# A list scheduler's durations for matmuls and DMA are replaced in a two-layer decoder trunk

## The chip, the cores and the metric

The kernel runs on one core of a Trainium2 chip. The metric is the device time of one execution in microseconds. Before the change the median of three runs is 997.61 us (995.69 to 997.91). One further execution was profiled; its numbers below are from that profile.

## The reference

A trunk of two layers works on one sequence of 256 tokens with 1024 channels in float32. Each layer is a half-step SwiGLU FFN, a token mixer and a second half-step FFN. The mixer of layer 0 is stick-breaking attention with 16 heads, that of layer 1 a gated linear recurrence (RG-LRU) with a width of 1280. Before each of the six sub-layers the input is normalized, scaled and shifted, and the result of the sub-layer is gated; scale, shift and gate come from a conditioning vector through a large matrix `mod_w` (2 layers x 1024 x 9216).

```python
c_act = jax.nn.silu(c)
for layer in range(DEPTH):
    mod = (c_act @ mod_w[layer] + mod_b[layer]).reshape(B, N_SUB, 3, D_MODEL)
    h, g = sublayer_input(x, norm_g[layer, 0], mod[:, 0])
    x = x + MACARON_W * g * swiglu(h, ffn_w_gu[layer, 0], ffn_w_down[layer, 0])
    h, g = sublayer_input(x, norm_g[layer, 1], mod[:, 1])
    ...
    x = x + g * y
    h, g = sublayer_input(x, norm_g[layer, 2], mod[:, 2])
    x = x + MACARON_W * g * swiglu(h, ffn_w_gu[layer, 1], ffn_w_down[layer, 1])
return rmsnorm(x, final_norm_g)
```

`sublayer_input` is `rmsnorm(x, g) * (1 + scale) + shift`. The weights are read once: some 250 MB, of which the conditioning matrix is 75 MB.

## The kernel before

*Arithmetic.* A product of float32 operands is made of three matmuls: each operand is split into a rounded high part and the remainder, and high x high, high x low and low x high are added up in PSUM. `Acc.group` (L514 to L534) issues such a group of three, all at L526: 128 x 128 weights against 256 tokens. A few products take float32 directly, in one instruction of four passes (`group32`, L543; the recurrence's gates, L1033; the sums of squares, L608).

*Weights.* They come in chunks of 1 MB (128 x 2048), which feed 16 groups. `load` (L482) reserves one of 3 `raw` buffers and issues the DMA (L472, on the SyncE queue). Then it splits the chunk in two halves of 1024 columns: ScalarE writes the high part `wh` (L497), VectorE the remainder `wl` (L500). There are 7 half-chunk buffers of either kind.

*Conditioning.* `mod_w` is not multiplied on TensorE. It is cut into 18 vectors (2 layers x 3 sub-layers x shift, scale, gate) of 8 tiles of 128 x 1024, 0.5 MB each: 144 tiles. `mod_tile` (L553) loads one into one of 3 `rawm` buffers, and VectorE multiplies it by `silu(c)` and sums along the row, in one instruction and a read of the accumulator (L564). When the 8 tiles of a vector are there, `mod_final` makes the shift (L577), the scale (L579, L582) or the gate (L579, L585). The 16 tiles of the first scale and shift go with the first weights. All others stand in a list in the order in which they are needed, beginning with the first gate, then the scale, shift and gate of attention, then the scale and shift of the second FFN: tiles 57 to 64 are that shift. `hook` (L1189) takes them off the list as the program is written down: in the first FFN 1.5 for every chunk of the up projection from the eighth on, and as much for every position of the down part, whose steps are two positions apart. A tile may be loaded, by the plan, once the last TensorE operation that was written down before it is done. That dependency orders the plan alone; on the chip a load waits for its buffer.

*Stages.* Each FFN has an up projection (22 chunks), then a down projection (`down`, L643, 11 chunks), whose last part finishes the eight 128-channel blocks of x one after the other: a residual addition (L666), a square (summed at L601) and a scaled copy `hx` of x, split again (`scaled`, L616 to L627). The next sub-layer begins with these copies (`up_first`, L705), before the sum of squares is known; two more columns carry the shift (L624), and the evictions apply the norm afterwards (L722, L723). So the first matmuls of a sub-layer need its scale and its shift. Attention works in eight pairs of heads: projections (L526, L836), masked scores (L900 and the paired products L912), a chain on ScalarE and VectorE, sums (L937, L939), values (L959), and then a down part of 4 chunks.

*The planner.* The program is written down as operations with an engine, a duration and buffers. `Program.schedule` (L165) then plays it through once, on the host, before anything is issued. Every operation gets a priority, its latest start by the durations of what depends on it; TensorE operations start from the running sum of their own durations (`nominal`, L115). The engine that can start first takes its most urgent operation; ScalarE and VectorE may hold still a little for a more urgent one that is about to become ready (`wait_for`, L227). A buffer is given out again when the plan says that its last user is done. At the end all operations are sorted by their planned start and issued in that order. The five queues, SyncE's DMA queue among them, are then worked off strictly in order, and semaphores keep the data right. A planned duration thus never delays an instruction by itself: it only decides what stands before what in each queue. The durations come from `c_act`, `c_dve`, `c_mm` and `c_dma` (L348 to L361), the delays between engines from the tables at L101 to L103. A DMA occupies the plan's single DMA engine for `c_dma` and lands 2000 ns (950 ns in the first loads) after that.

Of the kernel before, what the change touches and what calls it, by code (L numbers as in the profile page):

```python
# [14 lines left out]
P = 128  # L15
T = 256
# [337 lines left out]


def c_mm(n, passes=3):
    return passes * (max(n, 256) / 2.4 + 2.5)


def c_dma(n):  # L360
    return n * P * 4 / 360.0 + 20.0  # L361


@with_exitstack
def trunk(ctx, tc, xT, cb, par, modw, gu0, gu, wdn, qk, wv, wo, win, wri, wout, out):
# [3 lines left out]
    pr = Program()  # L369
# [101 lines left out]
    def dma(dst, src, n, w, after=(), lat=None):  # L471
        return pr.op("DMA", c_dma(n), lambda: sp.dma_start(dst(), src), w=w, after=after, lat=lat)  # L472

    def A(o, i, f, n, r, w, table=None, psum=False, ptr=0, after=(), **kw):
        def fn():
            act.activation(o(), i(), f, **{k: (v() if callable(v) else v) for k, v in kw.items()})  # L476
        return pr.op("ACT", c_act(n, psum, ptr), fn, r, w, after, table)

    def V(fn, n, r, w, cost=None, ptr=0):
        return pr.op("DVE", cost or c_dve(n) + 62.0 * ptr, fn, r, w)  # L480
# [26 lines left out]
    class Acc:  # L507
# [6 lines left out]
        def group(self, part, o, w, wc, xs, xc, stop, parts=(None,), passes=(0, 1, 2)):  # L514

            b = self.b
            start = not self.started
            self.started = True
            wh, wl = w
            xh, xl = xs  # L520

            def fn():
                seq = ((wh, xh), (wh, xl), (wl, xh))
                for n, i in enumerate(passes):
                    u, v = seq[i]
                    pe.matmul(o(b()), wc(u()), xc(v()), start=start and n == 0, stop=stop and n == len(passes) - 1,  # L526
                              skip_group_check=True)

            n = xs_n[0]
            rd = [wh, wl] + [(t, q) for t in (xh, xl) for q in parts]  # L530
            if not start:
                rd.append((b, "start"))
            wr = [(b, part)] + ([(b, "start")] if start else [])
            return pr.op("PE", c_mm(n, len(passes)), fn, rd, wr)  # L534
# [3 lines left out]
    def group32(acc, part, o, w, wc, x32, xc, n, stop):  # L538

        b = acc.b  # L540
        start = not acc.started
        acc.started = True
        pr.op("PE", c_mm(n, 4), lambda: pe.matmul(o(b()), wc(w()), xc(x32()), start=start, stop=stop, skip_group_check=True),  # L543
              [w, x32] + ([] if start else [(b, "start")]), [(b, part)] + ([(b, "start")] if start else []))
# [58 lines left out]
    def rstd(gen):  # L603
        qs = ssq.pop(gen)
        qs = qs if isinstance(qs, tuple) else (qs,)
        b = Buf(banks)
        for i, q in enumerate(qs):
            pr.op("PE", c_mm(T, 4), lambda i=i, q=q: pe.matmul(b()[:, :T], ones, q(), start=i == 0, stop=i == len(qs) - 1),  # L608
                  [q] + [b] * (i > 0), [b])
        r = Buf(rmsr)  # L610
        o = Buf(rstr)
        A(r, lambda: b()[:, :T], AF.Ln, T, [b], [r], table="lnexp", psum=True, ptr=1, bias=eps_t, scale=1.0 / D)
        A(o, r, AF.Exp, T, [r], [o], table="lnexp", scale=-0.5)
        return o
# [123 lines left out]
    def split(y, a, n):  # L738
        A(y[0], a, AF.Copy, n, [a], [y[0]])
        V(lambda: dve.tensor_tensor(y[1](), a(), f32(y[0]()), ALU.subtract), n, [a, y[0]], [y[1]])  # L740
# [66 lines left out]
    def attention(l, s, nxt, hook):  # L807
# [78 lines left out]
        def hd(ap, e):  # L886
            return ap[:, e * S : (e + 1) * S]

        def scores(f):

            qh, ql = qs.pop(f)
            zs[f] = Buf(banks), Buf(banks)
            u = Buf(F, 6, name=f"u{f}")

            def masked(e):
                b = zs[f][e]

                def fn():
                    diag = b().rearrange("p (e t) -> p e t", e=2)[:, :, :P]
                    pe.matmul(diag, ident, mask.rearrange("p (e t) -> p e t", e=2), start=True, stop=False,  # L900
                              skip_group_check=True)
                pr.op("PE", c_mm(T, 1), fn, [], [b])

            zb = zs[f]

            def products():

                for i, (kc, qc) in enumerate(((slice(T, T + P), slice(0, T)), (slice(T + P, 2 * T), slice(P, T)))):
                    for n, (v, w) in enumerate(((qh, qh), (qh, ql), (ql, qh))):
                        for e in range(2):  # L910
                            rows = slice(e * 64, (e + 1) * 64)
                            pe.matmul(zb[e]()[:, BL[i]], v()[rows, kc], w()[rows, qc], start=False,  # L912
                                      stop=i == 1 and n == 2, skip_group_check=True)

            for e in range(2):
                masked(e)
            pr.op("PE", 2 * c_mm(T), products, [qh, ql], list(zb))
            for e in range(2):
                A(lambda e=e: hd(u(), e), lambda b=zs[f][e]: b()[:, :S], AF.Abs, S, [zs[f][e]], [(u, e)], psum=True)
            A(u, u, AF.Exp, W2, [u], [u], table="lnexp", scale=-1.0)  # L920
            A(u, u, AF.Ln, W2, [u], [u], table="lnexp", bias=1.0)
            for e in range(2):
                V(lambda e=e, b=zs[f][e]: dve.scalar_tensor_tensor(hd(u(), e), b()[:, :S], 0.0, hd(u(), e), ALU.max, ALU.add),
                  S, [zs[f][e], (u, e)], [(u, e)])
            y = ws_[f] = Buf(R, 6, name=f"sh{f}"), Buf(R, 6, name=f"sl{f}")
            split(y, u, W2)
# [49 lines left out]
        for f in range(8):  # L976
            hook(f)
            q_proj(f)
            if f >= 2:
                values(f - 2)  # L980
            if f in (0, 1, 3, 5):
                v_proj((f + 1) // 2)
            if f >= 1:
                sums(f - 1)
            scores(f)
# [141 lines left out]
    def final():  # L1127
        q = rstd("end")

        def put(d0, n):  # L1130
            o = xall[:, d0 * T : (d0 + n) * T].rearrange("p (d t) -> p d t", d=n)
            V(lambda: dve.tensor_tensor(o, o, q().unsqueeze(1).to_broadcast([P, n, T]), ALU.mult), n * T,
              x[d0 : d0 + n] + [q], x[d0 : d0 + n])
            pr.op("DMA", c_dma(n * T), lambda: sp.dma_start(out[:, d0 : d0 + n, :], o), x[d0 : d0 + n], [])

        for d0, n in ((0, 1), (1, 1), (2, 2), (4, 2), (6, 1), (7, 1)):
            put(d0, n)
# [137 lines left out]
```

## Time and profile before

| | |
|---|---|
| runs, median | 997.61 us (995.69 to 997.91) |
| profiled execution | 996.92 us, span 994.8 us |
| mean granted TensorE clock | 0.996 |
| first group of the FFN (L526) | 13.7 us after the start |
| end of TensorE's last group | 986.0 us |
| DMA | 251.24 MB, 253 GB/s on average |
| conditioning tiles (L564) | 144, mean 1220 ns and 84 ns for the accumulator |
| wl splits (L500) | 328, mean 1210 ns |

Times within the profile count from its first instruction. PE is TensorE, PEld its weight load, DVE VectorE, ACT ScalarE, SPq the SyncE queue that issues all DMAs. The profile calls PE busy from a matmul's start to its modelled end, and those overlap; so how dense TensorE runs is better seen from the number of matmuls in a stretch of time than from its busy share. Durations of single instructions on VectorE overlap their successors a little, too: two L500 in a row take 2.35 us.

### The profile page before, as it was taken

What the parts mean: (1) busy time and instruction counts of PE and PEld (TensorE: products, weight loads), DVE (VectorE), ACT (ScalarE), POOL (GpSimd) and SP (SyncE); (2) the same over time, 40 slices, a digit from 0 to 9 for tenths busy, and PEclk for the clock granted to TensorE, in tenths of its full rate; (3) what the DMA queues carried; (4) which work ended last, traced back from release to release, by engine and by line L of the source; (5) the groups of instructions that cost most, each with busy time, mean ns of one, the idle gap of its engine ahead of it and who ended that gap; (6) DMA issues with size and microseconds to landing.
All of it is one profiled execution on the core that took longest, in us unless ns stands there. A gap on an engine that the chain in (4) does not pass through costs nothing.

```text
span 994.8 us, 19695 instructions
## 1 busy us (share of the span) xinstructions
PE 976.2 (98%) x8096; PEld 964.5 (97%) x8096; DVE 799.0 (80%) x1316; ACT 562.3 (57%) x902; POOL 2.2 (0%) x14
## 2 busy tenths in 40 slices
PE   6999999999999999999999999999999999999997
PEld 5999999999999899999999999999999999999996
DVE  7997888798888999888789988874997996555433
ACT  5475453478785754445366544443779785444333
POOL 0000000000000000000000000000000000000000
PEclk9999999999999999999999999999999999999999
DMA  8988899835556499889866888985244645555431
GB/s 332 352 325 315 331 333 330 334 136 203 198 206 236 170 341 336 331 327 341 326 246 253 329 327 333 343 324 212 108 134 164 254 175 209 204 175 186 166 115 43
DMA packets 48331, 251.24 MB, mean 253 GB/s; under 512 B 5489, under 2 KB 6129, under 8 KB 28530
## 3 DMA queue, kind: packets, MB, share of 16 engines
q1 hardware_dynamic: 48242, 249.99, 68.5%
q8 instruction: 63, 1.03, 0.4%
q14 instruction: 26, 0.21, 0.1%
HBM read 248.92 MB, written 1.05 MB: 251 GB/s over the span
## 4 chain that ended last, share of the span: by engine, by line
PE 95%; DVE 2%; DMA 1%; issue 0%; ACT 0%; SPq 0%; DVEq 0%
PE bank L526 89%; PE bank L836 2%; PE bank L1033 1%; PE bank L959 1%; DVE rawm L564 1%; PE bank L543 1%; PE bank L912 1%; PE bank L937 1%; DMA rawm<-in_modw 1%; DMA x<-in_xT 0%; PE bank L608 0%; PE bank L939 0%; DVE ssq L601 0%; DVE wl L500 0%; DVE x L666 0%
## 5 line engine op out<-in xcount | busy, mean ns | idle before, releaser
L526 PE MATMUL bank<-hx,wh 128*128 128x256 f32 (+1 forms) x3392 | 610.2, 283 | 5.1 <-ACT hx L476 4.8
L526 PEld LDWEIGHTS bank<-hx,wh 128*128 128x128 f32 x3392 | 522.3, 189 | 8.2 <-ACT hx L476 5.7
L497 ACT ACTIVATE wh<-raw 128x1024 fp32r<-128x1024 f32 (+1 forms) x328 | 336.8, 1046 | 340.1 <-PE bank L526 228.6
L500 DVE TENSOR_TENSOR wl<-raw,wh 128x1024 fp32r<-128x1024 f32 (+1 forms) x328 | 390.0, 1210 | 133.2 <-ACT wh L497 130.0
L526 PE MATMUL bank<-hx,wl 128*128 128x256 f32 (+1 forms) x1696 | 476.3, 281 | 0.0
L526 PEld LDWEIGHTS bank<-hx,wl 128*128 128x128 f32 x1696 | 321.2, 189 | 0.3 <-DVE wl L500 0.3
L526 PE MATMUL bank<-arenar,wh 128*128 128x256 f32 x1664 | 294.3, 280 | 0.0
L526 PEld LDWEIGHTS bank<-arenar,wh 128*128 128x128 f32 x1664 | 254.0, 188 | 0.1
L526 PE MATMUL bank<-arenar,wl 128*128 128x256 f32 x832 | 232.5, 279 | 0.0
L564 DVE SCALAR_TENSOR_TENSOR rawm<-rawm,cact 128x1024 f32<-128x1024 f32 x144 | 174.5, 1220 | 10.2 <-DMA rawm<-in_modw 10.0
L526 PEld LDWEIGHTS bank<-arenar,wl 128*128 128x128 f32 x832 | 156.3, 188 | 0.0
L476 ACT ACTIVATE arenar<-a 128x256 fp32r<-128x256 f32 x88 | 35.2, 404 | 4.9 <-DVE a L735 4.8
L740 DVE TENSOR_TENSOR arenar<-a,arenar 128x256 fp32r<-128x256 f32 x88 | 36.4, 419 | 0.5 <-ACT arenar L476 0.5
L735 DVE TENSOR_TENSOR a<-bank,sg 128x256 f32<-128x256 f32 x82 | 34.2, 419 | 0.1
L476 ACT ACTIVATE sg<-bank 128x256 f32<-128x256 f32 x82 | 30.2, 368 | 5.2 <-PE bank L526 1.7
L666 DVE SCALAR_TENSOR_TENSOR x<-bank,mf,x 128x256 f32<-128x256 f32 x48 | 22.1, 480 | 11.8 <-PE bank L526 11.6
L476 ACT ACTIVATE hx<-hpre,mf 128x256 fp32r<-128x256 f32 x48 | 23.2, 503 | 13.6 <-DVE mf L577 6.6
L476 ACT ACTIVATE hx<-x,mf 128x256 fp32r<-128x256 f32 x40 | 19.3, 504 | 20.3 <-DVE x L666 20.2
L636 DVE SCALAR_TENSOR_TENSOR hx<-hpre,mf,hx 128x256 fp32r<-128x256 f32 x48 | 22.8, 482 | 1.3 <-ACT hx L476 1.3
L634 DVE SCALAR_TENSOR_TENSOR hpre<-x,mf,rst 128x256 f32<-128x256 f32 x48 | 21.9, 482 | 2.3 <-ACT rst L476 1.9
L836 PE MATMUL bank<-wh,hx 128*128 128x256 f32 x128 | 23.7, 283 | 0.0
L476 ACT ACTIVATE arenaf<-arenaf 128x768 f32<-128x768 f32 (+1 forms) x31 | 21.9, 735 | 0.3
(97 smaller groups left out, 452.6 us busy)
## 6 DMA issues: line engine op xcount, KB each, us to landing
raw<-in_gu SPq DMA_DIRECT2D x79, 1024.0 KB, 4.9
rawm<-in_modw SPq DMA_DIRECT2D x144, 512.0 KB, 5.9
raw<-in_wdn SPq DMA_DIRECT2D x44, 1024.0 KB, 5.0
raw<-in_win SPq DMA_DIRECT2D x10, 1024.0 KB, 4.7
raw<-in_qk SPq DMA_DIRECT2D x8, 1024.0 KB, 4.8
raw<-in_gu SPq DMA_DIRECT2D x14, 512.0 KB, 6.7
raw<-in_wout SPq DMA_DIRECT2D x5, 1024.0 KB, 5.0
raw<-in_wv SPq DMA_DIRECT2D x4, 1024.0 KB, 4.7
```

Of the source, the lines that this page charges most:

```text
L476: act.activation(o(), i(), f, **{k: (v() if callable(v) else v) for k, v in kw.items()})
L497: act.activation(h()[:, :m], raw()[:, a : a + m], AF.Copy)
L500: dve.tensor_tensor(lo()[:, :m], raw()[:, a : a + m], f32(h()[:, :m]), ALU.subtract)
L526: pe.matmul(o(b()), wc(u()), xc(v()), start=start and n == 0, stop=stop and n == len(passes) - 1, skip_group_check=True)
L543: pr.op("PE", c_mm(n, 4), lambda: pe.matmul(o(b()), wc(w()), xc(x32()), start=start, stop=stop, skip_group_check=True), [w, x32] + ([] if ...
L564: dve.scalar_tensor_tensor(raw(), raw(), 1.0, cact(), ALU.mult, ALU.mult, accum_out=m()[:, t : t + 1])
L634: V(lambda: dve.scalar_tensor_tensor(hp(), x[d](), gs()[:, c], q(), ALU.mult, ALU.mult), T, [x[d], (gs, d), q], [hp], ptr=1)
L636: V(lambda: dve.scalar_tensor_tensor(lo()[:, :T], hp(), sh()[:, c], f32(hi()[:, :T]), ALU.add, ALU.subtract), T, [hp, (sh, d), hi], [lo], ...
L666: dve.scalar_tensor_tensor(x[d](), acc.b()[:, j * T : (j + 1) * T], gate()[:, d : d + 1], x[d](), ALU.mult, ALU.add)
L735: V(lambda: dve.tensor_tensor(a(), b()[:, T:], sg(), ALU.mult), T, [(b, (1, 0)), sg], [a])
L740: V(lambda: dve.tensor_tensor(y[1](), a(), f32(y[0]()), ALU.subtract), n, [a, y[0]], [y[1]])
L836: pe.matmul(o, u()[:, tb * P : (tb + 1) * P], v()[:, c0 : c0 + 256], start=start and n == 0, stop=k == KD - 1 and n == 2, skip_group_check ...
```

## The change

Three durations that the planner uses are replaced. A group of three matmuls is planned with 3 x 117.8 ns for up to 256 columns instead of 3 x (256/2.4 + 2.5) ns, a four-pass matmul with 432 ns instead of 4 x (256/2.4 + 2.5); for more columns both now grow in proportion. The paired score products are planned with 730 ns instead of two groups' worth. The DMA engine is planned with 400 bytes per nanosecond instead of 360. No operation, buffer or dependency is changed; the order in which the queues get their instructions, and the buffers of a ring that they are given, come out of `schedule` with the new durations.

```diff
 def c_mm(n, passes=3):
-    return passes * (max(n, 256) / 2.4 + 2.5)
+    return (432.0 if passes == 4 else 117.8 * passes) * max(n, 256) / 256
 
 
 def c_dma(n):
-    return n * P * 4 / 360.0 + 20.0
+    return n * P * 4 / 400.0 + 20.0
...
             for e in range(2):
                 masked(e)
-            pr.op("PE", 2 * c_mm(T), products, [qh, ql], list(zb))
+            pr.op("PE", 730.0, products, [qh, ql], list(zb))
```

## The prediction

> **What bounds the kernel now.** I read the engine totals first, then the chain that ended last, then a table of busy time over the stages, which I cut where the chain shows a sum-of-squares matmul (L608) or a gap.
>
> ```profile
> PE 976.2 (98%) x8096; PEld 964.5 (97%) x8096; DVE 799.0 (80%) x1316; ACT 562.3 (57%) x902; POOL 2.2 (0%) x14
> ...
> PE 95%; DVE 2%; DMA 1%; issue 0%; ACT 0%; SPq 0%; DVEq 0%
> ```
>
> ```profile
> 13.70:208.70 195.00, 195.00 (x1633) 194.62 (x1634) 171.22 (x285) 102.03 (x155) 0.00 (x0) 1.00 0.88 325
> 208.70:309.50 100.80, 100.80 (x843) 97.63 (x843) 86.39 (x142) 80.59 (x135) 0.00 (x0) 1.00 0.53 191
> 309.50:345.20 35.70, 32.23 (x247) 30.79 (x246) 33.61 (x76) 23.05 (x46) 0.00 (x0) 0.95 0.62 221
> 345.20:521.40 176.20, 176.16 (x1493) 176.16 (x1494) 153.76 (x241) 87.65 (x134) 0.00 (x0) 1.00 0.85 317
> 521.40:708.80 187.40, 187.40 (x1588) 187.35 (x1587) 155.05 (x247) 94.78 (x147) 0.00 (x0) 1.00 0.78 290
> 708.80:804.40 95.60, 95.60 (x748) 93.54 (x747) 87.03 (x163) 78.13 (x141) 0.00 (x0) 1.00 0.44 162
> 804.40:986.00 181.60, 181.60 (x1539) 181.54 (x1539) 100.86 (x141) 86.07 (x129) 0.00 (x0) 1.00 0.47 165
> ```
>
> The columns are the stretch and its length, then busy time and instructions of PE, weight load, DVE, ACT and POOL, the granted clock, the DMA share and GB/s. TensorE is busy throughout, so its busy time tells little; the number of matmuls per stretch tells more. A dense FFN stretch takes 176.20/1493 = 0.118 us per matmul, and 187.40/1588 and 181.60/1539 give the same. Three such passes are the 0.354 us that the new 117.8 x 3 stands for. At that rate the 1633 matmuls of the first stretch would need 192.7 us, 2.3 less than they take. Only one stretch is clearly loose: 309.5 to 345.2, the hand-over from attention to the next FFN. Its 247 matmuls need 29.1 us, plus about 0.5 for two longer L608 ones, and take 35.7: **6.1 us are lost there**. Together with the 13.7 us head and the 8.8 us tail that is everything a new order could win.
>
> What is late at that place is shown by the chain between 309 and 334 us, read with the clock:
>
> ```profile
> 311.51 0.77 DVE arenar L967 x2
> ...
> 312.31 1.25 DVE rawm L564 x2
> 313.58 5.50 DMA rawm<-in_modw
> 319.10 2.47 DVE rawm L564 x4
> 321.57 0.40 DVE hx L626
> 321.96 1.16 DVE rawm L564 x2
> 323.14 0.17 DVE mf L577
> ...
> 332.94 0.70 PE bank L608 x2
> ```
>
> ```profile
> 321.00:323.50 2.50, 0.38 (x4) 0.18 (x2) 2.46 (x7) 1.45 (x4) 0.00 (x0) 1.00 0.81 243
> 323.50:327.90 4.40, 4.30 (x22) 4.26 (x23) 4.40 (x15) 3.40 (x12) 0.00 (x0) 0.61 0.78 248
> ```
>
> The last conditioning tile is multiplied on VectorE (L564) at 321.96. Only then can the shift (L577) be formed, with it the two extra columns of the input of the next FFN, and the matmuls. TensorE stands still for some 2.5 us and then runs 4.4 us at a mean clock of 0.61, with 22 matmuls where 37 fit. So the stall is a backlog of conditioning tiles on VectorE. Where it comes from is seen when L564 alone is counted (its columns are PE, PEld, DVE, clock, DMA; a tile is two instructions) and where the DMA queue issued its loads:
>
> ```profile
> 59.00:86.00 27.00, 0.00 (x0) 0.00 (x0) 0.00 (x0) 1.00 0.81 299
> 86.00:140.00 54.00, 0.00 (x0) 0.00 (x0) 18.31 (x30) 1.00 0.89 333
> 140.00:195.00 55.00, 0.00 (x0) 0.00 (x0) 19.35 (x32) 1.00 0.90 331
> ```
>
> ```profile
> 208.70:254.00 45.30, 0.00 (x0) 0.00 (x0) 0.00 (x0) 1.00 0.50 180
> 254.00:302.00 48.00, 0.00 (x0) 0.00 (x0) 8.49 (x14) 1.00 0.57 207
> 302.00:323.00 21.00, 0.00 (x0) 0.00 (x0) 10.71 (x17) 1.00 0.66 231
> ```
>
> ```profile
> 193.92 3.02 SPq L472 DMA_DIRECT2D rawm<-in_modw  x3
> ...
> 255.62 8.91 SPq L472 DMA_DIRECT2D rawm<-in_modw  x2
> ```
>
> Three tiles were issued by 197 us, and VectorE did not touch one before 254. Seven were done in the next 48 us, and about nine were crowded into 302 to 323.
>
> **The change part by part.** No instruction of the chip is added or taken away, so its direct price is zero; all of it is order. One weight chunk is 1 MB and feeds 16 groups.
>
> Matmul price. A group goes from 3 x (256/2.4 + 2.5) = 327.5 to 353.4 ns, a chunk from 5240 to 5654. The dense stretches say 16 x 0.354 = 5.66 us, so the plan now keeps the chip's pace; before, it ran 8% ahead. A four-pass group goes from 437 to 432 ns, which I cost at nothing: it concerns some 80 instructions. The paired scores go from 655 to 730 ns, where the trace has
>
> ```profile
> 219.36 0.84 PE bank L912 x12
> ```
>
> so eight of them stay about 0.1 us short each, 0.9 us in the stage.
>
> DMA price. 1 MB goes from 2933 to 2641 ns, a conditioning tile of 0.5 MB from 1476 to 1331. The highest rate in the trace bounds the truth:
>
> ```profile
> 25.00:50.00 25.00, 25.00 (x211) 24.85 (x209) 24.73 (x48) 11.62 (x14) 0.00 (x0) 1.00 0.95 351
> ```
>
> 351 GB/s at a share of 0.95 is 369 at a share of 1, hence 2.84 and 1.42 us by that estimate. The old price is 3 to 4% high, the new one 6 to 7% low.
>
> Both together set **how many conditioning tiles the plan can load per chunk**. Old: (5240 - 2933)/1476 = 1.56. New: (5654 - 2641)/1331 = 2.26. The first FFN offers tiles at 1.5 per chunk while it goes up, then 3 per chunk in its down part. The trace shows the old budget at work: 15 tiles in 54 us (9.5 chunks) are 1.57 per chunk, 16 in 55 us (9.7) are 1.65, though 3 were offered there. By 208.7 us 48 tiles were multiplied, and 64 are needed before the next FFN; 16 + 52 = 68 were offered by then. So 16 fell into attention and the hand-over (20 + 12 instructions of L564, 1.2 us a tile).
>
> With the new prices I count 16 early tiles, up to 21 in the 14 chunks going up, and 11 x 2.26 = 25 going down: 62, and 59 if the DMA engines hold only (5.66 - 2.84)/1.42 = 1.99 per chunk. Two to five of the 16 remain, and 11 to 14 tiles, 13 to 17 us of VectorE, leave attention and the hand-over. Even if the tiles came no earlier, attention has room: VectorE is busy 86.39 of 100.80 us there. The old plan held that stage to be 8% shorter, so about 7 of those 14.4 us did not exist for it; now they do, enough for six tiles. Nine were left after 302 us. I therefore take the backlog to be gone, and what is late next is the ordinary hand-over. The one at 521.4 us shows its price as next to nothing, since the dense rate holds on both sides of it.
>
> I let 1.0 us of the 6.1 stay for the waits of the normalization and the first evictions, which did not hang on a tile. **Sum:** the profiled execution took 996.92 us for a span of 994.8. 996.9 - 5.1 = 991.8. The median of the runs is 997.61, 0.7 above the profiled one, so 992.5 is the forecast in its terms. The bounds are 6.1 us won (990.8, or 991.5 by the median) and nothing won.
>
> Where the new order puts more into the FFN down parts, two covers hide it. VectorE has two splits and 2.26 tiles there, 2 x 1.13 + 2.26 x 1.2 = 5.0 of 5.65 us. The DMA engines are asked for 2.84 + 2.26 x 1.42 = 6.05 us per chunk of 5.65, 0.40 too much, 4.4 us over 11 chunks. What hides that is the weight ring: seven half-chunk buffers are 7 x 2.83 = 19.8 us of TensorE, and it is mostly full, since the splits wait for TensorE to release a buffer far more than for data:
>
> ```profile
> ACT wh L497 <- PE bank L526: 228.6, 116, 3.7
> ...
> ACT wh L497 <- DMA raw<-in_gu: 26.3, 18, 4.7
> ```
>
> The Trainium skill ("DMA: Bandwidth & Descriptors", section "Where 436 GB/s comes from") speaks against the new DMA price: it gives about 358 GB/s per core as the limit for loads from HBM. The 351 GB/s of the row above stays under it. By that figure a chunk would ask for 2.93 + 2.26 x 1.46 = 6.24 us, and a down part be 6.5 us too dear instead of 4.4, still less than the ring holds.
>
> **The rivals.**
>
> *The backlog stays.* A tile has a late due time, so VectorE prefers other work while any is at hand; three loaded tiles lay for 57 us with VectorE idle a seventh of the stage. If the plan again gives its new gaps to softmax work it waits for, tiles come in time of need only, and the stall keeps its 6 us: 997.6, give or take 2. Against it: the number loaded before attention was set by the DMA budget, which grows by 45%.
>
> *Overbooked DMA, slower.* In the down parts of the three FFNs that load tiles, weights arrive 0.40 us late per chunk. Nothing shows while the ring is ahead; from the chunk at which it holds less than the shortfall, TensorE waits. 33 chunks x 0.40 are 13.2 us at most; with the hand-over mended, 997.6 - 5.1 + 13.2 = 1005.7. For it: a DMA share of 0.90 already in 140 to 195. Against it: the 228.6 us above.
>
> *The stall moves, slower.* Tiles that now land near 200 us are put among the residual and scaling work of the first hand-over, where VectorE is nearly full:
>
> ```profile
> 200.00:225.00 25.00, 25.00 (x215) 24.69 (x214) 23.25 (x54) 19.68 (x37) 0.00 (x0) 1.00 0.37 131
> ```
>
> Three or four tiles at 1.2 us there pass its slack, and TensorE stops and cools as at 321 us, another 6 us. If the attention backlog also stays: 1003.7.
>
> **How the numbers follow.** Backlog gone: 0.55, at 992.5, its own range 990.8 to 995. Backlog stays: 0.17, at 997.6. Overbooked DMA: 0.18, at 999 to 1006. Moved stall: 0.10, at 1000 to 1004. Of this kernel a difference of 0.2%, 2 us, can be told from none. Faster is the first case, 0.55; the same 0.17; slower 0.28. The range 990.5 to 1002.5 holds the first two and some half of the slower ones.
>
> **What would show it.** L564 should have over 55 tiles done by 208.7 us instead of 48, fewer than three after 302, and no gap of its loads from 197 to 255. The stretch from 309.5 should hold 0.118 us per matmul and the clock 1.00. The prediction is wrong if the tile counts stay and the stall with them, if TensorE waits for a wl or wh buffer in a down part while the DMA share is near 0.95, or if a dip of the clock appears at another hand-over.

## The result, and the profile after

| | median, us | range | profiled execution | ratio to before (95% interval) |
|---|---|---|---|---|
| before | 997.72 | 995.69 to 997.91 | 996.92 | |
| after | 1014.16 | 1009.31 to 1014.80 | 1014.80, span 1013.1 | 1.0159 (1.0125 to 1.0193) |

The kernel became 1.6% slower; faster had been forecast. The same table of busy time by stage, cut at the hand-overs of the new profile (stretch and length, then busy time and instructions of PE, weight load, DVE, ACT and POOL, clock, DMA share, GB/s):

```profile
13.40:215.60 202.20, 198.20 (x1630) 196.25 (x1631) 180.84 (x306) 99.56 (x151) 0.00 (x0) 0.99 0.91 339
215.60:317.20 101.60, 101.60 (x848) 98.14 (x847) 95.71 (x161) 83.54 (x147) 0.00 (x0) 1.00 0.64 223
317.20:335.30 18.10, 18.10 (x154) 18.10 (x154) 17.11 (x36) 13.77 (x25) 0.00 (x0) 1.00 0.55 192
335.30:494.20 158.90, 158.90 (x1348) 158.84 (x1347) 140.24 (x233) 76.25 (x119) 0.00 (x0) 1.00 0.89 331
494.20:546.40 52.20, 41.59 (x305) 39.52 (x303) 45.33 (x76) 23.80 (x38) 0.00 (x0) 0.90 0.81 289
```

At 0.118 us per matmul the third row is dense (154 x 0.118 = 18.2): the loss of 6.1 us behind attention is gone. The price stands in two other rows. The first stretch needs 192.3 us for its 1630 matmuls and takes 202.2, 9.9 lost where 2.3 were lost before. The last needs 36.0 for 305 and takes 52.2, 16.2 lost where nothing was. So 7.6 + 16.2 - 6.1 = 17.7 us, against 18.3 between the two spans.

The conditioning tiles (L564; two instructions a tile) did move as forecast. In the first stretch of the prediction there are now

```profile
13.70:208.70 195.00, 0.00 (x0) 0.00 (x0) 67.23 (x111) 1.00 0.93 347
```

111/2, some 55 tiles, where the profile before had 92/2 = 46; two more come earlier in both. What went wrong with them is in the groups and the waits of the new page. A group's row gives its busy time and mean, then the idle time of its engine just before it and who ended that:

```profile
L564 DVE SCALAR_TENSOR_TENSOR rawm<-rawm,cact 128x1024 f32<-128x1024 f32 x144 | 174.8, 1220 | 38.6 <-DMA rawm<-in_modw 38.3
L526 PEld LDWEIGHTS bank<-arenar,wl 128*128 128x128 f32 x832 | 157.0, 189 | 9.5 <-DVE wl L500 9.5
...
rawm<-in_modw SPq DMA_DIRECT2D x144, 512.0 KB, 6.3
```

and the same two groups in the page before:

```profile
L564 DVE SCALAR_TENSOR_TENSOR rawm<-rawm,cact 128x1024 f32<-128x1024 f32 x144 | 174.5, 1220 | 10.2 <-DMA rawm<-in_modw 10.0
L526 PEld LDWEIGHTS bank<-arenar,wl 128*128 128x128 f32 x832 | 156.3, 188 | 0.0
```

VectorE stood 38.3 us before tiles that had not landed, 10.0 before the change, and TensorE waited for low parts of weights, which VectorE makes. How the one leads to the other can be read in VectorE's own timeline around the long stall:

```profile
505.20 1.23 DVE L564 SCALAR_TENSOR_TENSOR rawm<-rawm,cact 128x1024 f32<-128x1024 f32 x1 [2.68 <-DMA rawm<-in_modw]
...
506.82 1.23 DVE L564 SCALAR_TENSOR_TENSOR rawm<-rawm,cact 128x1024 f32<-128x1024 f32 x1 [0.38 <-DMA rawm<-in_modw]
...
507.97 2.36 DVE L500 TENSOR_TENSOR wl<-raw,wh 128x1024 fp32r<-128x1024 f32 x2
...
514.49 2.36 DVE L500 TENSOR_TENSOR wl<-raw,wh 128x1024 fp32r<-128x1024 f32 x2
```

and in the two other queues of the same stretch, ScalarE's and SyncE's:

```profile
504.06 2.01 ACT L497 ACTIVATE wh<-raw 128x1024 fp32r<-128x1024 f32 x2 [5.44 <-DMA raw<-in_wdn]
509.54 2.00 ACT L497 ACTIVATE wh<-raw 128x1024 fp32r<-128x1024 f32 x2 [3.48 <-DMA raw<-in_gu]
```

```profile
496.46 0.33 SPq L472 DMA_DIRECT2D raw<-in_wdn  x1
496.84 2.52 SPq L472 DMA_DIRECT2D rawm<-in_modw  x2
501.42 0.33 SPq L472 DMA_DIRECT2D raw<-in_gu  x1
501.80 5.00 SPq L472 DMA_DIRECT2D rawm<-in_modw  x2
```

The last weight chunk of the down projection was late twice. ScalarE waited 5.44 us for its load and made the high parts from 504.06 us. The low parts came only at 507.97, behind two tile products that waited for their DMAs. For the chunk after it the two times are 509.54 and 514.49, and TensorE's longest gap lies there, 5.05 us from the start of one matmul at 510.7 to that of the next. A tile's product in turn frees the buffer that the next tile load on SyncE waits for, and behind that load stands the next weight chunk. Three queues, each worked in order, form a loop.

### The profile page after: what moved, and what is told of

It is laid out like the page before. It is cut to its first block, busy times and chain, and to the rows that moved or that the text cites. A ratio compares the mean times of both kernels' runs of the same rounds, so it can differ in the third digit from the quotient of the medians.

```text
span 1013.1 us, 19729 instructions
## 1 busy us (share of the span) xinstructions
PE 983.4 (97%) x8096; PEld 968.9 (96%) x8096; DVE 796.2 (79%) x1316; ACT 559.2 (55%) x902; POOL 2.2 (0%) x14
## 4 chain that ended last, share of the span: by engine, by line
PE 80%; DMA 10%; DVE 7%; ACT 2%; issue 1%; SPq 0%; DVEq 0%; ACTq 0%
PE bank L526 73%; DMA rawm<-in_modw 6%; DMA raw<-in_gu 3%; PE bank L836 2%; DVE rawm L564 2%; DVE wl L500 2%; ACT wh L497 1%; PE bank L1033 1%; PE bank L959 1%; PE bank L543 1%; PE bank L912 1%; DVE x L666 1%; DVE hx L626 1%; PE bank L937 1%; DMA x<-in_xT 1%
## 5 line engine op out<-in xcount | busy, mean ns | idle before, releaser
L500 DVE TENSOR_TENSOR wl<-raw,wh 128x1024 fp32r<-128x1024 f32 (+1 forms) x328 | 389.5, 1207 | 136.8 <-ACT wh L497 136.5
L564 DVE SCALAR_TENSOR_TENSOR rawm<-rawm,cact 128x1024 f32<-128x1024 f32 x144 | 174.8, 1220 | 38.6 <-DMA rawm<-in_modw 38.3
L740 DVE TENSOR_TENSOR arenar<-a,arenar 128x256 fp32r<-128x256 f32 x88 | 36.4, 417 | 1.0 <-ACT arenar L476 1.0
L735 DVE TENSOR_TENSOR a<-bank,sg 128x256 f32<-128x256 f32 x82 | 34.0, 417 | 0.1
L836 PE MATMUL bank<-wh,hx 128*128 128x256 f32 x128 | 23.8, 284 | 0.0
```

The lines of the kernel that those rows point to most:

```text
L500: dve.tensor_tensor(lo()[:, :m], raw()[:, a : a + m], f32(h()[:, :m]), ALU.subtract)
L564: dve.scalar_tensor_tensor(raw(), raw(), 1.0, cact(), ALU.mult, ALU.mult, accum_out=m()[:, t : t + 1])
L735: V(lambda: dve.tensor_tensor(a(), b()[:, T:], sg(), ALU.mult), T, [(b, (1, 0)), sg], [a])
L836: pe.matmul(o, u()[:, tb * P : (tb + 1) * P], v()[:, c0 : c0 + 256], start=start and n == 0, stop=k == KD - 1 and n == 2, skip_group_check ...
```

## The experiments

Five explanations were tried. A: the new order asks the DMA engines for more bytes than they bring. B: the slower matmul price makes the weights late. C: the three tile buffers are asked for more turns than they can make. D: VectorE has too much work. E, which came up after the first eight kernels: VectorE is held up in its order, because the plan takes a tile to be there earlier than it is. The plan's tile lands 1.33 + 2.0 = 3.3 us after its DMA starts; the trace has 6.3 us from issue to landing.

All edits are against the changed kernel unless told otherwise. Each ratio is to runs of the kernel before that were made on the same chip along with it. A profile shows one execution. Those of e1, e9 and e11 took 1005.28, 994.83 and 1007.84 us, 4 to 6 us above the medians, so their losses look larger in the profiles.

**The two prices apart.**

```diff
# e1: matmul and score prices alone
-    return n * P * 4 / 400.0 + 20.0
+    return n * P * 4 / 360.0 + 20.0
# e2: DMA price alone
-    return (432.0 if passes == 4 else 117.8 * passes) * max(n, 256) / 256
+    return passes * (max(n, 256) / 2.4 + 2.5)
...
-            pr.op("PE", 730.0, products, [qh, ql], list(zb))
+            pr.op("PE", 2 * c_mm(T), products, [qh, ql], list(zb))
```

> The new matmul and score prices with the old DMA price of 360 bytes per ns. Theory A (the plan overbooks the DMA queue): it can plan (5654 - 2933)/1476 = 1.84 conditioning tiles per weight chunk instead of 2.26, under the 1.99 that the DMA engines deliver by the highest rate of the profile before. The stalls of the changed kernel near 50, 210 and 495 to 546 us go, the hand-over after attention stays mended, and the time is about 992 to 995 us. Theory B (the slower matmul price itself makes weights late): the long stall near 500 us stays, 1008 to 1014 us.

Measured: 1000.95 us, ratio 1.0036 (1.0019 to 1.0053).

> The new DMA price with the old matmul and score prices. Theory A: (5240 - 2641)/1331 = 1.95 tiles per chunk are planned, close to what the DMA engines deliver, and the plan holds the chip to be 8% faster than it is; most of the long stall is gone, 997 to 1004 us. Theory B: without the slower matmul price there is no long stall, and the time is that of before, about 997 us, or below.

Measured: 998.61 us, 1.0010 (0.9998 to 1.0022). Neither theory had e1 right. The matmul price alone loses a little and leaves a shorter stall near 500 us (a gap of 4.2 us at 504.7); the DMA price alone loses nothing that can be told. That is a sum, though: the profile of e2 has no gap behind attention any more, but only 310 matmuls between 13.5 and 60 us, where the one before has 373, and 63 matmuls are 7.4 us. Together the prices lose 16. So it is no sum of two prices but something that tips over. The score price was not tried by itself.

**Half the bytes, or a fourth buffer, with the same order of every queue.**

```diff
# e3
-        load_ = dma(raw, modw[l, (s * 3 + w) * KD + t], D, [raw], after, lat)
+        load_ = pr.op("DMA", c_dma(D), lambda: sp.dma_start(raw()[:, : D // 2], modw[l, (s * 3 + w) * KD + t][:, : D // 2]),
+                      w=[raw], after=after, lat=lat)
...
-            dve.scalar_tensor_tensor(raw(), raw(), 1.0, cact(), ALU.mult, ALU.mult, accum_out=m()[:, t : t + 1])
+            two = lambda ap: ap.rearrange("p (e t) -> p e t", e=2)
+            h = raw()[:, : D // 2].unsqueeze(1).to_broadcast([P, 2, D // 2])
+            dve.scalar_tensor_tensor(two(junk[:, :]), h, 1.0, two(cact()), ALU.mult, ALU.mult, accum_out=m()[:, t : t + 1])
# e4: mods holds the three planned buffers and one more
+    class Spread(Buf):
+        def __call__(self):
+            return mods[taken.setdefault(self, len(taken) % 4)]
...
-        raw = Buf(modr)
+        raw = Spread(modr)
```

> The order of the changed kernel on every queue, but each load of a conditioning tile brings only the first half of it (256 KB), and VectorE multiplies that half twice over, so that its work is as long as before; the conditioning values are then wrong. Theory A (too many bytes for the DMA engines): the stalls near 210 and 495 to 546 us go, 990 to 995 us. Theory C (a tile buffer comes free too late, since a load and the product that frees its buffer take longer than planned, and the weight loads queue behind the waiting load): a load of half the size still takes most of its 6 us to land, so at least half of the 18 us near 500 us stays, 1003 to 1010 us.

Measured: 992.16 us, 0.9952 (0.9936 to 0.9969).

> The order of the changed kernel on every queue, planned with three buffers for conditioning tiles, but the tiles are spread over four buffers, so that a load waits for the product four tiles back instead of three. Room for it comes from moving the three buffers of the FFN's activations into the phase arena and the buffer of the norm's logarithm onto one that only the recurrence uses. Theory A: bytes and order are the same, so the DMA engines are as late as before, 1008 to 1015 us. Theory C: the turnaround of the buffers rises by a third, the queue no longer stops, and the time falls to 992 to 998 us.

Measured: 997.04 us, 0.9988 (0.9974 to 1.0002): 17 us less than the changed kernel with the same order and the same bytes. **A falls** as the cause of the long stall. The stretch of the second FFN ahead of the stall, first after the change, then with four buffers:

```profile
350.00:495.00 145.00, 144.86 (x1229) 144.65 (x1228) 126.34 (x208) 64.80 (x101) 0.00 (x0) 1.00 0.92 343
495.00:546.00 51.00, 40.67 (x298) 39.01 (x298) 44.16 (x75) 23.40 (x37) 0.00 (x0) 0.90 0.82 289
```

```profile
350.00:495.00 145.00, 145.00 (x1233) 145.00 (x1232) 131.64 (x209) 66.15 (x96) 0.00 (x0) 1.00 0.94 359
495.00:546.00 51.00, 48.09 (x378) 46.73 (x378) 48.81 (x90) 29.61 (x51) 0.00 (x0) 0.97 0.75 279
```

The DMA engines could do 359 GB/s; after the change they were used for 343. And what SyncE waited for between 350 and 495 us, after the change and with four buffers (in e4 L500, L564 and L740 have the numbers L509, L573 and L758):

```profile
SPq L472 <- DVE rawm L564: 71.0, 35, 4.6
SPq L472 <- DVE arenar L740: 35.1, 17, 4.7
SPq L472 <- DVE wl L500: 13.3, 7, 3.0
```

```profile
SPq L481 <- DVE arenar L758: 59.8, 16, 7.8
SPq L481 <- DVE wl L509: 34.8, 9, 5.9
SPq L481 <- DVE rawm L573: 17.0, 13, 2.5
```

After the change the queue stood mostly before tile buffers; with a fourth it stands before weight buffers, that is, it is ahead of TensorE. Every one of these waits ends with an instruction on VectorE, which frees the tile buffers and the weight buffers alike. Half the bytes mend the time as well, but a tile then lands sooner too (a median of 4.8 us between 440 and 520 against 7.8 after the change), so e3 by itself decides nothing.

**The plan's landing time, VectorE's work, and the fourth buffer under the old order.**

```diff
# e5
-                mod_tile(*key, t, after=[pr.last_pe])
+                mod_tile(*key, t, after=[pr.last_pe], lat=5000.0)
# e6
-            dve.scalar_tensor_tensor(raw(), raw(), 1.0, cact(), ALU.mult, ALU.mult, accum_out=m()[:, t : t + 1])
+            h = slice(0, D // 2)
+            dve.scalar_tensor_tensor(raw()[:, h], raw()[:, h], 1.0, cact()[:, h], ALU.mult, ALU.mult,
+                                     accum_out=m()[:, t : t + 1])
# e7: e4 with the three prices of the kernel before
# e8: e4 with the DMA price of 360
```

> The changed kernel with one planned number more set to a traced one: a conditioning tile taken off the list lands 5000 ns after its DMA time instead of 2000 (the profile of the changed kernel has 6.3 us from issue to landing, 1.3 of them the transfer). Three buffers are kept. Theory C: the plan now knows the turnaround of the three buffers, loads fewer tiles per chunk in the second FFN, and the weight loads are no longer queued behind a tile that waits; 992 to 1000 us. If only bytes counted (theory A), the prices of the transfers are unchanged and the stall near 500 us stays, 1006 to 1014 us.

Measured: 995.16 us, 0.9974 (0.9962 to 0.9986).

> The order of the changed kernel on every queue; full tiles are loaded, but VectorE multiplies only the first half of each, 0.6 us instead of 1.2; the conditioning values are then wrong. Theory C: the turnaround of a buffer falls by 0.6 of some 9 us, so the stall near 500 us shrinks by a few us only, 1004 to 1012 us. Theory D (VectorE has too much to do in the new order): the stalls go, 990 to 996 us.

Measured: 996.43 us, 0.9995 (0.9976 to 1.0014), well below what C expected and just above what D did.

> The fourth tile buffer of the earlier run with the prices and hence the order of the kernel before. Theory C: before, weights were not late anywhere, so nothing is won in the FFNs, and the hand-over at 309 to 345 us depends on VectorE's order; 994 to 998 us. If instead the fourth buffer is worth as much under any order, some 980 us.

Measured: 996.27 us, 0.9984 (0.9975 to 0.9993): a fourth buffer is worth about 1 us where no queue is held up.

> The fourth tile buffer with the new matmul and score prices and the old DMA price: the hand-over is mended by the order, and the milder load of tiles fits four buffers. Theory C: all stalls but the first go, 990 to 993 us. If the stall that was left with the matmul prices alone (1001 us) is one of bytes, it stays, 998 to 1002 us.

Measured: 992.19 us, 0.9942 (0.9930 to 0.9955); its profile has no gap of half a microsecond on TensorE between 20 and 980 us.

e6 is the miss that told most. D cannot be the answer in its plain form: in the first 25 us of the stall VectorE is busy for 18.5 only, and e4 and e5 leave its work as it is. But halving a product helped more than the buffers' turns explain. In e5, moreover, SyncE stands even longer before tile buffers, with no stall:

```profile
SPq L472 <- DVE rawm L564: 82.6, 48, 4.6
```

What e5 does change is VectorE's idle time before tiles, in the same 145 us, after the change and in e5:

```profile
DVE rawm L564 <- DMA rawm<-in_modw: 18.5, 14, 3.1
```

```profile
DVE rawm L564 <- DMA rawm<-in_modw: 1.6, 3, 0.9
```

After the change 126.3 us busy and 18.5 us held up are 144.8 of 145: VectorE's queue was full, and it splits the weights. That is theory E, and the last kernels were made for it.

**Tests of E.**

```diff
# e9: e5 with the DMA price of 360
# e10
-             lambda k: (ys[k], slice(0, T)), 2, lambda c: hook(NF + 2 * c))
+             lambda k: (ys[k], slice(0, T)), 2, lambda c: hook(NF + c))
# e11: against the kernel before
-                mod_tile(*key, t, after=[pr.last_pe])
+                mod_tile(*key, t, after=[pr.last_pe], lat=500.0)
# e12
-                mod_tile(*key, t, after=[pr.last_pe])
+                mod_tile(*key, t, after=[pr.last_pe], lat=3500.0)
```

> Three buffers, the new matmul and score prices, the old DMA price, and a conditioning tile taken off the list lands 5000 ns after its DMA time in the plan. Theory C: the plan asks for at most 1.84 tiles per chunk, under the 2.04 that three buffers with a measured loop of 8.3 us from issue to release can turn over (3 x 5.66/8.3), and it knows the loop; no stall near 500 us. The small stalls between 27 and 60 us, which only the kernels with the DMA price of 400 show, should be gone as well: 991 to 994 us. If the three buffers were too few under any order with the new matmul price, it is no better than the 1001 us of the matmul prices alone.

Measured: 990.89 us, 0.9926 (0.9914 to 0.9939), the fastest of all; four of five runs lie between 990.0 and 991.4, one at 994.8.

> The prices of the change, but the down parts of the FFNs take half as many conditioning tiles off the list (the tiles are then loaded in later stages; all are computed). In the queue order, 13 tiles instead of 18 stand between the weight chunks of the second down part. Theory C: fewer turns of the three buffers are asked for where the weights ran late, so the stall near 500 us shrinks by more than half, 993 to 1002 us; the small stalls before 60 us stay. If the order of VectorE's or ScalarE's other work were the cause, the time stays at 1008 to 1014 us.

Measured: 996.72 us, 0.9987 (0.9974 to 1.0000).

> The kernel before with one planned number made worse on purpose: a conditioning tile taken off the list is planned to land 500 ns after its DMA time instead of 2000. Matmul and DMA prices, and so the number of tiles asked for per weight chunk, stay as before. Theory E (VectorE works its queue in order; a tile's product that the plan places before the tile has landed holds up the weight splits behind it): VectorE's waits for tiles between 350 and 495 us rise from 3.9 to over 12 us, and the time to 1000 to 1012 us. Theory C (too many turns of the tile buffers are asked for): as many are asked for as before, 995 to 999 us.

Measured: 1001.81 us, 1.0051 (1.0036 to 1.0066).

> The changed kernel with the tiles planned to land 3500 ns after their DMA time, halfway between the 2000 of the change and the 5000 that gave 995 us. As many tiles stand before the last weight chunk of the second FFN as in the changed kernel, 124. Theory E: VectorE's waits for tiles between 350 and 495 us come between the 18.5 and the 1.6 us of those two, and the time is 996 to 1004 us. Theory C: as many turns of the buffers as in the changed kernel are asked for, 1008 to 1014 us.

Measured: 1000.12 us, 1.0021 (0.9996 to 1.0047).

The planned landing time alone moves the kernel before by +5 us (e11) and the changed one by 14 (e12) and 19 (e5), in each case the way E says; C expected no change in e11 and none in e12. But e4, e5 and e7 to e10 came out within 1 us of what C expected, too, and do not tell C from E. Nor does the number of tiles decide: between the sixth weight load of the second FFN and its last, SyncE's queue holds 48 tiles in e12 and 43 in e2, without a stall, and 43 in e1 and 47 after the change, with one. VectorE's idle time before tiles between 350 and 495 us, with its busy time there, how long ScalarE's splits stood there before buffers that TensorE had not released ("ring full"), and the matmuls done in the 51 us after it, from the views of waits and of stretches:

| kernel | busy | before tiles | sum of 145 | ring full | matmuls 495 to 546 | median, us |
|---|---|---|---|---|---|---|
| before | 125.9 | 3.9 | 129.8 | 47.5 | 431 | 997.7 |
| after | 126.3 | 18.5 | 144.8 | 10.0 | 298 | 1014.2 |
| e1, matmul prices | 122.9 | 21.5 | 144.4 | 28.3 | 352 | 1001.0 |
| e2, DMA price | 133.0 | 6.5 | 139.5 | 46.4 | 423 | 998.6 |
| e3, half the bytes | 136.1 | 4.1 | 140.2 | 43.5 | 428 | 992.2 |
| e4, four buffers | 131.6 | 12.3 | 143.9 | 52.2 | 378 | 997.0 |
| e5, landing 5000 | 132.7 | 1.6 | 134.3 | 52.9 | 432 | 995.2 |
| e6, half products | 107.7 | 36.0 | 143.7 | 44.3 | 413 | 996.4 |
| e7, before + four buffers | 125.9 | 0.7 | 126.6 | 50.4 | 432 | 996.3 |
| e8, e1 + four buffers | 129.6 | 9.0 | 138.6 | 55.8 | 428 | 992.2 |
| e9, e1 + landing 5000 | 129.7 | 1.4 | 131.1 | 53.3 | 432 | 990.9 |
| e10, half the offer | 122.8 | 11.6 | 134.4 | 47.0 | 422 | 996.7 |
| e11, before + landing 500 | 125.4 | 17.5 | 142.9 | 31.8 | 420 | 1001.8 |
| e12, landing 3500 | 136.8 | 7.3 | 144.1 | 54.3 | 422 | 1000.1 |

The three kernels that did fewer than 400 matmuls in the last stretch had a full VectorE queue and over 12 us of it held up. The reverse does not hold, for the sum does not tell a wait that holds up weight splits from one behind which nothing was due. The ring tells them apart in part: e12's queue is as full, and e6, with halved products, stood 36.0 us before tiles, but their rings stayed full for 54.3 and 44.3 us and little was lost; the least full rings are those of the changed kernel and of e1. In e4 the ring was full until 495, and the shorter stall comes after it (a gap of 2.0 us at 513.4).

e11 bears E out in VectorE's waits and in the time, but not in the place. It loses most at the hand-overs ahead of attention and behind it: 348 matmuls between 180 and 225 us against 384 before, and 335 against 361 between 300 and 350, with a gap of 5.2 us at 326.2 (2.5 at 321.1 before). The planned landing time also moves tile loads among the weight loads on SyncE (45 instead of 47 in the second FFN for e5), so the two ends of the loop, late loads and a held-up VectorE, are not wholly apart in any of these kernels. What is shown is that the planned landing time decides whether the stall comes; which end of the loop weighs more is not.

A second loss is not explained by this. In the first 60 us the kernels with a DMA price of 400 may fall behind the others; e5 and then e9, which differ in that price alone:

```profile
13.50:60.00 46.50, 44.05 (x337) 41.98 (x337) 41.81 (x82) 22.64 (x29) 0.00 (x0) 1.00 0.96 346
```

```profile
13.50:60.00 46.50, 45.98 (x365) 45.75 (x366) 45.62 (x87) 24.91 (x34) 0.00 (x0) 1.00 0.98 357
```

28 matmuls are 3.3 us, most of the 4.3 between the two medians. e3 and e4, with half the bytes and with a fourth buffer, have the same price and do 364 and 366 there. Why some are late and others not stays open.

## Why the prediction was wrong

*What bounds the kernel*: right. The 6.1 us behind attention were a backlog of tiles, and the new order cleared it as forecast: some 57 tiles by 208.7 us, a dense hand-over. The other signs came only in part: no tile load was issued between 210 and 252 us, and seven products began between 302 and 323 us instead of fewer than three, but six of them complete a gate (L585), for which no matmul waited. Two of the signs that it had named for being wrong came as well, the wait for `wl` in a down part and dips of the clock at other hand-overs. e9, which has little else wrong, is 7.1 us faster than the runs of before beside it (997.97 to 990.89), where 5.1 had been forecast for that hand-over.

*Tiles per chunk*: the direction was right. The queue after the change holds 47 tiles between the sixth weight chunk of the second FFN and its last, 27 chunks on, 1.74 per chunk; before it held 35, 1.30. Neither reaches the 2.26 and 1.56 of the prediction; why is not shown. Nor did the tiles go where the prediction had them, into the down part: from its first weight load to its last the queue holds 18, 17 before, and in the up projection ahead of it 29, 18 before.

*The covers*: this step failed: "two covers hide it. VectorE has two splits and 2.26 tiles there, 2 x 1.13 + 2.26 x 1.2 = 5.0 of 5.65 us." That counts VectorE's work, not its waits. In the 145 us before the long stall, up projection and down part together, its work was 126.3 us, 87%, within the 88% of that sum; waits of 18.5 us before tiles filled the rest. The row that warns of them stood in the page before, in the list of DMA issues:

```profile
rawm<-in_modw SPq DMA_DIRECT2D x144, 512.0 KB, 5.9
```

512 KB of `in_modw` took 5.9 us to land, and the plan has 3.3 to 3.5. The prediction asked of each new duration whether it is true, and not of the one beside it that stays wrong. Before, the two old prices kept tile loads few (35 in the stretch counted above; either new price alone makes 43), and VectorE met a late tile 14 times, for 10.0 us; after, 35 times, for 38.3.

*The ring*: "mostly full" was true of the old order. Between 350 and 495 us ScalarE waited as follows, first before the change, then after it:

```profile
ACT wh L497 <- PE bank L526: 47.5, 25, 3.6
...
ACT arenar L476 <- DVE a L735: 1.2, 2, 1.0
```

```profile
ACT arenar L476 <- DVE a L735: 52.7, 17, 6.2
ACT wh L497 <- DMA raw<-in_wdn: 13.1, 4, 4.8
ACT wh L497 <- PE bank L526: 10.0, 10, 1.5
```

After the change its splits waited only 10.0 us for TensorE to release a buffer. In the up projection ScalarE stood behind VectorE's L735, and from 472 us on each chunk's split waited 3 us or more for its load. The 19.8 us of cover were used up there, unseen by TensorE, which was dense until 494. This fits a stall that breaks out late and all at once.

*The rivals*: the overbooked DMA had the place, the down parts with weights late, and even the point from which it decides. Its resource was wrong, since e4 carries the same bytes in the same order and is 17 us faster. Its price of 13.2 us at most was below the 23.8 lost in the two stretches. The moved stall happened too, at 208.8 us: between 180 and 225 us the changed kernel does 335 matmuls, 384 before, and 49 are 5.8 us, near the 6 us that this rival was given. The rivals had been weighed one against the other, and two of them came together. The size of a gain had been bounded by a loss measured in the profile; the bound of a loss counted transfers alone, and the range was drawn too near to the gain.

*What beats both*: the new matmul and score prices, the old DMA price, and tiles planned with their traced landing time (e9), 0.74% faster than before.

## What to carry to other kernels

In a plan that only fixes the order of in-order queues, durations work as a set: making some of them true can lay bare another that is false, here the time from a load's issue to its use. When a queue is said to hide extra work, add its waits to its work; an engine at 87% that is placed before late loads can be full. And a ring that covers a shortfall hides it from the bound engine until it is empty, so look at who waits for the ring's slots, not at the bound engine, to see a stall coming.

## What the runs showed of the hardware that was not expected

The highest rate of one 25 us slice after the change was

```profile
425.00:450.00 25.00, 25.00 (x214) 25.00 (x214) 22.73 (x39) 10.35 (x16) 0.00 (x0) 1.00 0.97 377
```

377 GB/s, and e12 held 371 GB/s over the 145 us from 350. At a full share these would be 389 (377 at 0.97) and 382 (371 at 0.97), where the prediction took 369. It had also weighed a limit of about 358 GB/s per core from the Trainium skill ("DMA: Bandwidth & Descriptors", section "Where 436 GB/s comes from"). The traces do not agree with that limit: 377 and 371 lie above it.

How long a load takes to land is no constant. The median of the 512 KB loads between 440 and 520 us was 6.4 us before, 7.8 after the change and 6.0 in e12, and that of the 1 MB loads of the down part 5.0, 6.7 and 7.0. The rate in that stretch does not order them: it was 311, 343 and 358 GB/s. What does is not shown. With the 2.0 us that the plan adds to a transfer it had 4.9 us for a 1 MB load before, which fits, but only 3.3 to 3.5 us for 512 KB, which does not.
